# A third shared PSUM bank for the pairs' mixers, and a price for changing the first partition on VectorE and ScalarE in the order model

## The chip, the core and the metric

One core of a Trainium2 chip. The metric is the device time of one execution in microseconds (us). The kernel is written with a list scheduler of its own: Python code keeps a model of when each engine is free and when each result is ready, and it emits every engine's instructions in the order that this model picks. On the chip each engine runs its list in that fixed order and waits where a result isn't there yet.

## The reference, cut to what matters

One layer of a hybrid decoder, for 528 prompt rows (16 meta rows and 512 tokens) and 64 sample rows (8 sequences of 8). All inputs are fp32.

```python
z = einsum('btd,dn->btn', x, w_in)               # 2048 -> 4224 + 4096 columns
o_a, s_a, shift = rwkv7_mixer(z[..., :4224])      # 16 heads x 64: token shift, decay, scan over time, group norm, gate
o_b, s_b = retention_mixer(z[..., 4224:])         # 8 heads x 128: rotary, blocks of 128, group norm, gate
h = einsum('btc,cd->btd', concat([o_a, o_b]), w_out)
y = layer_norm(ALPHA * x + h)
```

The outputs are y for prompt and sample rows, the two mixers' final states, and the last projected rows. The scan of the first mixer is computed in chunks of 64 rows: inside a chunk with matmuls and a triangular inverse, and from chunk to chunk with a recurrence on a 64 x 64 state for each head.

## The kernel before, in words

**Projections.** The work goes by eight pairs p. Pair p takes two heads of the first mixer (units k, r, v, g of kind A) and one head of the second (units q, k, v, g of kind B). A unit is 128 columns of w_in for all 592 rows: 16 contraction tiles of 128, two halves of the rows (272, 258 or 256 columns, then 320), and three matmuls each (high x high, high x low, low x high parts of the fp32 values). So a unit has 96 projection matmuls and a pair 768. They read weights `wh`, `wl` (high and low part of a weight chunk) and `XH`, `XL` (those of x), and write `pj`, PSUM banks 0 and 1. In the lists the eight banks are named bank_115 to bank_122, so bank_115 and bank_116 are the projections'. Each chunk of weights, 128 x 512, comes by DMA into `raw`, ScalarE writes `wh` from it, and VectorE writes `wl` = raw - wh.

**Mixers between the projections.** The mixers' own matmuls are put between the projection matmuls, one small group at a time. Generators write them step by step: `gen_a` (first mixer, up to the chunks), `gen_c` (its recurrence over nine chunks, inside gen_a), `gen_u` (inverse of 32 x 32 blocks, VectorE with DMA), `gen_s` (sample rows), `gen_f` (group norm and gate), `gen_b` (second mixer). `act`, `tt`, `stt` and `ts` are the ScalarE and VectorE instructions, and every one of them has line 363 in the profile, every matmul line 386, and every transpose line 392. Names of tiles tell them apart:
- The recurrence (`gen_c`) does for each chunk c: ScalarE `SF` (two halves of 64 partitions), matmul AR x Y, ScalarE `RHS` (two halves), matmul TT x RHS, VectorE product with `N` into ZZ, matmul BT x ZZ, and VectorE, twice on 64 partitions, the next Y from `bank,FT,SF`. These three matmuls are called the Y step, the RHS step and the BT step below. They alone are a chain: each waits for ScalarE or VectorE work on the result of the one before.
- `gen_s` has eight ScalarE copies into `RSv`, each of 64 partitions, then the transpose `CT,RSv`, and later two matmuls of 64 x 512.
- `gen_b` has eight ScalarE copies of 32 partitions (`XH<-RT` and `RT<-RT`) ahead of two matmuls `XH 128x512` whose contraction has 96 rows.
- `gen_a` begins with the matmuls `LWw` and `LWa` (decay and gain), which need two banks for the two halves of the rows, each written twice and read by ScalarE in between.

**What sets the order.** `Order` holds a clock for each engine and, for each piece of memory, when it is written and read. `Op.ns` is an instruction's cost in the model: for ScalarE 51 ns (input in PSUM) or 93 ns plus 0.833 ns a column, for VectorE 68 ns plus 1.04 ns a column, and more for operands that are pointers. `ready` adds a lag for each dependence: 150 ns from VectorE and 180 ns from ScalarE, and `SLACK` more when the instruction that waits is a matmul. After every projection matmul `pump` looks at the jobs that are live, in order of priority, and puts out each job's next instructions: a mixer's matmul only when the model has its operands ready by now. `ensure` forces what the next projection can't do without.

**Banks.** `take` waits until the list `free` holds as many banks as asked for, and `give` puts them back. `free` begins with m0 and m1 (bank_117 and bank_118). sq (bank_119) serves the first transposes and, at the end, the first output cell; ob (bank_120) is the recurrence's output; r0 and r1 (bank_121 and 122) are gen_b's.

**Output.** After the pairs, w_out is applied in 20 cells of 128 rows x 512 columns, the first of them in bank_119, and the layer norm follows.

Of the kernel before, what the change touches and what calls it, by code (L numbers as in the profile page):

```python
# [28 lines left out]
NPAIR = 8  # L29
RAW_BUFS = 3  # L30
HI_BUFS = 4
SLACK = 200.0
AHEAD = -300.0
RUN = 1200.0
DRAIN = 90.0
LAND = 2400.0
LAND_BIG = 2400.0
LD = 4
# [4 lines left out]
SHARE = "ggggggggggggggdddddd"  # L43
LATE = 5
EARLY = 14
BACKLOG = {0: 4000.0, 1: 1000.0, 2: 500.0, 3: 300.0, 4: 100.0}

_CSPEC = [("ident", 128), ("ind", 2), ("mS", 64), ("mSs", 64), ("mQ", 64), ("mQs", 64),
# [62 lines left out]
class Op:  # L111


    __slots__ = ("eng", "ns", "reads", "writes", "emit", "size")

    def __init__(self, eng, ns, reads, writes, emit, size=None):
        self.eng, self.ns, self.emit, self.size = eng, ns, emit, size
        self.reads, self.writes = [_box(a) for a in reads], [_box(a) for a in writes]


def _box(ap):


    t = ap.tensor
    dims = ap.ap
    if ap.space == bass.MemoryType.DRAM:
        return (t.name, 0, 1, ap.offset, ap.offset + sum((n - 1) * abs(s) for s, n in dims) + 1)
    if ap.space == bass.MemoryType.PSUM:
        return (t.name, -1, 0, 0, 1)
    pitch = 1  # L130
    for d in t.shape[1:]:
        pitch *= d
    p0, c0 = divmod(ap.offset, pitch)
    return (t.name, p0, p0 + dims[0][1], c0, c0 + sum((n - 1) * abs(s) for s, n in dims[1:]) + 1)


def _is_ap(x):
# [19 lines left out]
class Order:  # L157
# [6 lines left out]
    def __init__(self):  # L164
        self.clock = {k: 0.0 for k in ("PE", "DVE", "ACT", "POOL", "SP", "AQ", "DMA")}
        self.mem = {}
        self.job = None
        self.live = []
        self.stage = {}
        self.first = 0.0  # L170
        self.shape = (128, 128)
        self.tiles = [[0.0, 0.0] for _ in range(16)]
        self.issued = (0.0, 0.0)

    def lag(self, src, dst, raw):
        if src == dst:
            return 130.0 if raw and src in ("DVE", "ACT", "POOL") else 0.0
        return self.LAG[src] + SLACK * (dst == "PE")

    def ready(self, op):  # L180
# [7 lines left out]
                        t = max(t, end + self.lag(eng, op.eng, w and not isw))  # L188
        return t

    def emit(self, op):
        ns = op.ns
        start = max(self.clock[op.eng], self.ready(op))
        end = start + ns
        if op.eng == "PE":
            end = self.array(op, self.ready(op))
        self.clock[op.eng] = end
        if op.eng in ("SP", "AQ"):
            end = max(end + 1300.0, self.clock["DMA"]) + op.size / 270.0
            self.clock["DMA"] = end  # L200
            end += LAND if op.size < 2e5 else LAND_BIG
        for boxes, w in ((op.reads, False), (op.writes, True)):
            for n, p0, p1, c0, c1 in boxes:
                l = self.mem.setdefault(n, [])
                if len(l) > 40:
                    t = self.clock["PE"] - 3000.0
                    l[:] = [x for x in l if x[6] > t]
                l.append((p0, p1, c0, c1, w, op.eng, end))
        op.emit()

    def array(self, op, ready):
# [4 lines left out]
        if shape != self.shape:  # L216
            idle = max(e for _, e in self.tiles) + DRAIN
            for x in self.tiles:
# [68 lines left out]
    def pump(self):  # L287
        more = True
        limit = self.clock["PE"] + RUN
        while more:  # L290
            more = False
            for j in list(self.live):
                while self.flushed(j):
# [3 lines left out]
                    if op.eng == "PE":  # L297
# [5 lines left out]
                        elif r > now:  # L303
                            break
                    elif r > now + AHEAD - LATER * (j.name == "load") or self.clock[op.eng] > now + BACKLOG[j.prio * (op.eng != "SP")]:
                        break
# [61 lines left out]
class TensorEngine:  # L368
# [3 lines left out]
    def place(self, lhsT, out, whole):  # L372

        _, p0, p1, _, _ = _box(lhsT)
        c0, m = out.offset // out.tensor.shape[1], _cols(lhsT)
        up = lambda n: 32 if n <= 32 else 64 if n <= 64 else 128
        r, c = up(p1 - p0), 128 if whole else up(m)
        return (r, c), [4 * i + j for i in range(p0 // 32, (p0 // 32) + r // 32) for j in range(0 if whole else c0 // 32, (0 if whole else c0 // 32) + c // 32)]
# [28 lines left out]
def kernel(ctx, tc, x_prompt, x_sample, state_rwkv, state_shift, state_ret, meta_tokens, w_in, w_out,  # L407
# [3 lines left out]
    od = Order()  # L411
    V, A, G = (Engine(e, k, od) for e, k in ((nc.vector, "DVE"), (nc.scalar, "ACT"), (nc.gpsimd, "POOL")))
# [133 lines left out]
    bank = [psum.tile([128, 512], F32, name=f"bank{i}") for i in range(8)]  # L546
    pj = [bank[0], bank[1]]
    m0, m1, sq, ob, r0, r1 = bank[2:]
    free = [m0, m1]

    o_d = dram.tile([16, 128, 576], F32, name="o_d")
    lt_d = [dram.tile([4, 10, 32, 32], F32, name=f"lt_d{i}") for i in range(2)]
# [23 lines left out]

    def give(*b):
        od.call(lambda: free.extend(b))

    lock = [1]  # L580

# [419 lines left out]
    def span(u, half):  # L1001

        if half:
            return H0, H1
        t0 = {"A": 14 * (u[2] in "rg"), "B": 16 * (u[2] in "qg"), "L": 0}[u[0]]
        return t0, H0 - t0
# [88 lines left out]
    j_in = len(chunks)  # L1095
    for i in range(EARLY):
        events.append(("out", len(chunks), 0, i, (0, 1)))
        chunks.append(("out", korder[i], 0))
    for n in range(4):
        for i in range(KO):  # L1100
            events.append(("out", len(chunks), n, i, (2, 3, 4) if n == 0 and i < EARLY else tiles))
            chunks.append(("out", korder[i], n))
    j_one = j_in + EARLY + KO
    last = {ev[1]: e for e, ev in enumerate(events)}
# [48 lines left out]
    with tc.manual_schedule():  # L1153
# [192 lines left out]
        for e, ev in enumerate(events):  # L1346
            stage["event"] = e
            j = ev[1]
            if ev[0] == "in":
                _, j, u, half, q, ui = ev  # L1350
                kind, p, s = u
                if half == 0 and q == 0:
                    if kind == "A" and s == "k":
                        od.start(f"A{p}", gen_a(p), 1)
                    if kind == "B" and s == "q":
                        od.start(f"B{p}", gen_b(p), 3)
                if q == 0 and ui:
                    od.ensure("evac", 2 * ui - 1 + half)
                if ui == 0 and half == 1 and q == 0:
                    od.ensure("x", 99)  # L1360
                od.ensure("split", j + 1)
                t0, n = span(u, half)
                b, jb = pj[half], part[j]
                for kk in range(4):
                    kt = 4 * q + kk
                    w = slice(128 * kk, 128 * kk + 128)
                    for i, (a_, x_) in enumerate(((WH[jb], xh), (WH[jb], xl), (WL[jb], xh))):
                        mm(b[:, :n], a_[:, w], x_[:, kt, t0:t0 + n], start=(kt == 0 and i == 0), stop=(kt == 15 and i == 2))
                        if kk == 3 and i == 2:
                            stage["event"] = e + 1  # L1370
                            if q == 3:
                                stage["proj"] = 2 * ui + half + 1
                        od.pump()
            else:
                _, j, n, ki, some = ev
                od.ensure("o", ki + 1)
                if ki == 0:
                    if n == 0 and 4 in some:
                        od.ensure(f"B{NPAIR-1}", 99)
                        od.ensure("shift", 99)  # L1380
                    if n:
                        od.ensure(f"F{NPAIR-1}", 99)
                        od.ensure("cell", 5 * n + 5 - 8)
                od.ensure("split", j + 1)
                work = [(t, ki, part[j]) for t in some]
                if n == 3 and ki >= KO - HELD:
                    late += work[1:]
                    work = work[:1]
                    if ki == KO - 1:
                        work += sorted(late, key=lambda w: w[0])  # L1390
                for iw, (t, k_, jb) in enumerate(work):
                    b = obank[5 * n + t]
                    if k_ == 0 and b in pj:
                        od.ensure("evac", 2 * len(units) - 1 + pj.index(b))
                    tok = slice(128 * t, 128 * t + 128)
                    if t < 4:
                        todo = [(b, xo[:, k_, tok], WH[jb]), (b, xl[:, k_, tok], WH[jb]), (b, xo[:, k_, tok], WL[jb])]
                    else:
                        todo = [(b, xo[:, k_, tok], WH[jb]), (b[0:64], xo[:, k_, 512:576], WL[jb])]
                        if k_ == KO - 1:  # L1400
                            todo.reverse()
                    for i, (b_, x_, w_) in enumerate(todo):
                        end = i == len(todo) - 1
                        mm(b_, x_, w_, start=(k_ == 0 and i == 0), stop=(k_ == KO - 1 and end))
                        if k_ == KO - 1 and end:
                            stage["out"] = 5 * n + t + 1
                        if iw == len(work) - 1 and end:
                            stage["event"] = e + 1
                        od.pump()
# [41 lines left out]
```

## Time and profile before

| | |
|---|---|
| median of 3 runs | 1382.36 us (1382.06 to 1383.02) |
| profiled execution | 1382.55 us, span 1380.8 us |
| TensorE matmul busy | 1331.4 us, 96% of the span |
| TensorE weight load busy | 1230.1 us, 89% |
| VectorE busy | 884.0 us, 64% |
| ScalarE busy | 644.7 us, 47% |
| DMA | 139.79 MB, 101 GB/s in the mean |
| granted TensorE clock | 0.991 in the mean |

PE is the row of the matmuls, PEld that of the weight loads, which run ahead of the matmuls. Their busy times overlap, since a matmul's record lasts longer than the distance to the next one's start. Where PEld is idle and a releaser is named, the array's next weights waited for that engine. The pairs follow each other at 139.2 us. "Position" is used below for a place in TensorE's list: the number of projection matmuls that stand ahead of it in its pair, 0 to 767.

### The profile page before, as it was taken

How to read it: one execution, taken by the hardware profiler on the slowest of the kernel's cores; microseconds unless marked ns; L12 is line 12 of the kernel's file. 1: busy time of each engine (PE TensorE's matmuls, PEld its weight loads, DVE VectorE, ACT ScalarE, POOL GpSimd, SP SyncE). 2: the span in 40 equal slices, each digit the busy share in tenths (PEclk: the TensorE clock that was granted, in tenths of full speed). 3: DMA queues.
4: the chain of work that ended last, by engine and by line, in shares of the span. 5: the costliest groups of instructions: out<-in, count | busy, mean ns of one | idle time of the engine just before them, and what ended most of it. 6: DMA issues, size and time to landing. Idle time of an engine off the chain costs nothing.

```text
span 1380.8 us, 26964 instructions
## 1 busy us (share of the span) xinstructions
PE 1331.4 (96%) x10392; PEld 1230.1 (89%) x10392; DVE 884.0 (64%) x2158; ACT 644.7 (47%) x1519; POOL 72.5 (5%) x131
## 2 busy tenths in 40 slices
PE   7999999999999999999999999999999999999993
PEld 6999899989998999899989998999899987777782
DVE  5774677566766676667666765676567658624347
ACT  4534564366336633663356435643564366512121
POOL 0000000000000000000000000100010001000024
PEclk9999999999999999999999999999999999999997
DMA  7343224322432243224322432243224347654313
GB/s 238 87 109 90 69 74 118 94 66 72 118 87 73 66 123 85 75 65 120 84 81 64 118 80 81 63 118 85 80 62 120 88 138 214 195 166 117 98 48 122
DMA packets 232342, 139.79 MB, mean 101 GB/s; under 512 B 58668, under 2 KB 212102, under 8 KB 231238
## 3 DMA queue, kind: packets, MB, share of 16 engines
q1 hardware_dynamic: 232214, 138.08, 35.3%
q8 instruction: 81, 1.33, 0.4%
q14 instruction: 47, 0.39, 0.1%
HBM read 119.30 MB, written 18.74 MB: 100 GB/s over the span
## 4 chain that ended last, share of the span: by engine, by line
PE 81%; DVE 9%; ACT 6%; issue 3%; DMA 0%; POOL 0%; DVEq 0%; SPq 0%; ACTq 0%; POOLq 0%
PE bank L386 77%; DVE RW L363 5%; PE bank L392 4%; DVE wl L363 1%; ACT RW L363 1%; ACT SF L363 1%; ACT XH L363 1%; DVE MOM L363 1%; ACT RT L363 1%; ACT RHS L363 1%; ACT wh L363 1%; DVE RT L363 1%; ACT RSv L363 1%; DVE SHT L363 1%; DVE XL L363 0%
## 5 line engine op out<-in xcount | busy, mean ns | idle before, releaser
L386 PE MATMUL bank<-XH,wl 128*128 128x320 f32 (+3 forms) x2080 | 634.0, 305 | 2.1 <-DVE wl L363 2.1
L386 PE MATMUL bank<-XL,wh 128*128 128x320 f32 (+3 forms) x2080 | 629.1, 302 | 0.0
L386 PE MATMUL bank<-XH,wh 128*128 128x320 f32 (+3 forms) x2080 | 627.5, 302 | 1.2 <-ACT wh L363 1.2
L386 PEld LDWEIGHTS bank<-XL,wh 128*128 128x128 f32 x2080 | 391.9, 188 | 7.9 <-issue 6.3
L386 PEld LDWEIGHTS bank<-XH,wl 128*128 128x128 f32 x2080 | 392.9, 189 | 6.0 <-DVE wl L363 3.6
L386 PEld LDWEIGHTS bank<-XH,wh 128*128 128x128 f32 x2080 | 392.8, 189 | 3.0 <-ACT wh L363 1.4
L363 DVE TENSOR_TENSOR wl<-raw,wh 128x512 fp32r<-128x512 f32 x292 | 201.4, 691 | 203.0 <-ACT wh L363 200.1
L363 ACT ACTIVATE wh<-raw 128x512 fp32r<-128x512 f32 x292 | 184.1, 631 | 205.3 <-PE bank L386 178.6
L363 DVE TENSOR_TENSOR RW<-RW 120x84 f32<-120x84 f32 (+27 forms) x558 | 149.9, 272 | 19.5 <-ACT RW L363 4.0
L386 PE MATMUL bank<-RW 32*32 32x32 f32 (+6 forms) x1904 | 146.8, 242 | 2.9 <-DVE RW L363 2.0
L386 PEld LDWEIGHTS bank<-RW 32*32 32x32 f32 (+4 forms) x1904 | 108.9, 145 | 28.0 <-DVE RW L363 9.0
L363 ACT ACTIVATE RW<-bank 128x512 f32<-128x512 f32 (+8 forms) x218 | 93.2, 438 | 47.2 <-PE bank L392 33.3
L363 ACT ACTIVATE RT<-bank 64x320 f32<-64x320 f32 (+9 forms) x122 | 47.7, 398 | 126.4 <-DVE RT L363 102.7
L363 ACT ACTIVATE SF<-RW,FT 64x64 f32<-64x64 f32 x144 | 49.7, 345 | 71.1 <-DVE RW L363 69.2
L386 PE MATMUL bank<-more,XH 128*128 128x512 f32 (+1 forms) x250 | 75.9, 395 | 0.0
L363 ACT ACTIVATE RW<-bank,OMM 128x272 f32<-128x272 f32 (+1 forms) x66 | 33.2, 502 | 68.9 <-PE bank L386 67.4
L386 PE MATMUL bank<-wh,XH 128*128 128x512 f32 x157 | 62.0, 396 | 0.0
L392 PE MATMUL bank<-CT,RW 128*128 128x128 f32 (+2 forms) x348 | 53.7, 282 | 8.2 <-DMA RW<-in_x_prompt_dram 7.5
L386 PE MATMUL bank<-wl,XH 128*128 128x512 f32 (+1 forms) x157 | 61.6, 394 | 0.0
L386 PEld LDWEIGHTS bank<-more,XH 128*128 128x128 f32 (+1 forms) x250 | 45.6, 183 | 12.4
L363 DVE TENSOR_TENSOR RW<-bank,N 64x128 f32<-64x128 f32 x80 | 22.5, 282 | 46.8 <-PE bank L386 45.7
L392 PEld LDWEIGHTS bank<-CT,RW 128*128 128x128 f32 (+2 forms) x348 | 41.2, 139 | 10.4 <-issue 7.5
(154 smaller groups left out, 1397.3 us busy)
## 6 DMA issues: line engine op xcount, KB each, us to landing
raw<-in_w_in_dram SPq DMA_DIRECT2D x259, 256.0 KB
raw<-in_w_out_dram SPq DMA_DIRECT2D x48, 256.0 KB
CT<-in_w_out_dram SPq DMA_DIRECT2D x30, 256.0 KB
RT<-in_state_ret_dram SPq DMA_DIRECT2D x8, 512.0 KB
out_dram<-RT SPq DMA_DIRECT2D x8, 512.0 KB
RW<-in_x_prompt_dram SPq DMA_DIRECT2D x16, 256.0 KB
out_dram<-RW SPq DMA_DIRECT2D x16, 256.0 KB
RW<-o_d SPq DMA_DIRECT2D x14, 288.0 KB
```

The costliest lines, as they stand in the source:

```text
L363: self.order.submit(Op(self.key, self.cost(name, n, kw, psum), reads, [out], lambda: f(*args, **kw)))
L386: lambda: self.eng.matmul(out, lhsT, rhs, start=start, stop=stop), (passes, move, load, shape, tiles)))
L392: lambda: self.eng.transpose(out, in_, ident), (1, move, _cols(in_) / 1.2, shape, tiles)))
```

## The change

It has three parts. `free` begins with three banks, so the mixers may also hold sq, and a job `keep` takes that bank out of the list from the last pair's unit g on, before the output phase writes it. In the model, an instruction on VectorE or ScalarE starts 110 ns later (`SWITCH`) than its engine is free when the first partitions of its output and first input aren't those of the engine's instruction before. And `SLACK`, the extra lag ahead of every matmul, goes from 200 to 100 ns. No instruction is added or removed: the model puts the same ones in another order.

```diff
-SLACK = 200.0
+SLACK = 100.0
...
+SWITCH = 110.0
...
+KEEP = ("A", 7, "g")
...
     def __init__(self, eng, ns, reads, writes, emit, size=None):
         self.eng, self.ns, self.emit, self.size = eng, ns, emit, size
+        self.rows = tuple(_row(a) for a in writes + reads[:1])
...
+def _row(ap):
+    pitch = 1
+    for d in ap.tensor.shape[1:]:
+        pitch *= d
+    return ap.offset // pitch
...
+    def switch(self, op):
+
+        return SWITCH * (op.eng in ("DVE", "ACT") and self.rows.get(op.eng) != op.rows)
+
     def emit(self, op):
         ns = op.ns
-        start = max(self.clock[op.eng], self.ready(op))
+        start = max(self.clock[op.eng] + self.switch(op), self.ready(op))
+        self.rows[op.eng] = op.rows
...
-    free = [m0, m1]
+    free = [m0, m1, sq]
...
+    def gen_keep(b):
+
+        while not any(x is b for x in free):
+            yield
+        free[:] = [x for x in free if x is not b]
+        yield
...
+                    if (kind, p, s) == KEEP:
+                        od.start("keep", gen_keep(sq), 0)
...
+                od.ensure("keep", 99)
```

**First place: ScalarE and TensorE in the last unit of pair 3.** ScalarE's list from the copy of the sample state (`RW<-bank 128x512`) on, before:

```order
L363 ACTIVATE RW<-bank_117 128x512
L363 ACTIVATE RT<-bank_121,CT 32x128
L363 ACTIVATE XH<-RT 32x128 x2
L363 ACTIVATE RT<-RT 32x128 x2
L363 ACTIVATE XH<-RT 32x128 x2
L363 ACTIVATE RSv<-bank_117 64x4x8
L363 ACTIVATE RT<-RT 32x128 x2
L363 ACTIVATE RSv<-bank_117 64x4x8 x2
L363 ACTIVATE wh_102<-raw_101 128x512
```

The same place after the change:

```order
L380 ACTIVATE RW<-bank_119 128x512
L380 ACTIVATE RT<-bank_121,CT 32x128
L380 ACTIVATE RT<-bank_115 128x256
L380 ACTIVATE XH<-RT 32x128 x2
L380 ACTIVATE RSv<-bank_119 64x4x8
L380 ACTIVATE RT<-RT 32x128 x2
L380 ACTIVATE RSv<-bank_119 64x4x8
L380 ACTIVATE XH<-RT 32x128 x2
L380 ACTIVATE RSv<-bank_119 64x4x8
L380 ACTIVATE SF<-RW,FT_83 64x64
L380 ACTIVATE wh_102<-raw_101 128x512
```

The copies themselves stand much as they did, a little more mixed; the sample rows now use the third bank. What moved is TensorE's list, where the matmuls that wait for them stand. Before, in the second weight chunk of that half unit (wh_103), from position 741 on:

```order
L386 MATMUL bank_121<-XH 128x512
L386 MATMUL bank_118<-RW 128x128
L386 MATMUL bank_116<-XH,wh_103 128x320
L386 MATMUL bank_116<-XL,wh_103 128x320
L392 MATMUL bank_117<-CT,RSv 128x128
L386 MATMUL bank_116<-XH,wl_107 128x320
L386 MATMUL bank_116<-XH,wh_104 128x320
L386 MATMUL bank_116<-XL,wh_104 128x320
L386 MATMUL bank_118<-RHS,RW 66x128
```

After, in its fourth chunk (wh_105), from position 758 on:

```order
L403 MATMUL bank_118<-RHS,RW 66x128
L403 MATMUL bank_121<-XH 128x512
L403 MATMUL bank_116<-XH,wl_109 128x320
L403 MATMUL bank_116<-XH,wh_105 128x320
L403 MATMUL bank_116<-XL,wh_105 128x320
L403 MATMUL bank_116<-XH,wl_109 128x320
L403 MATMUL bank_118<-RW 128x128
L403 MATMUL bank_119<-CT,RSv 128x128
```

The XH matmul went from position 741 to 758, the RSv transpose from 743 to 762, and the RHS step of that chunk from 746 to 758.

**Second place: TensorE at the next pair's LWw matmuls.** Before, they come right after the recurrence's last group (`64x64 x32`), at position 97:

```order
L386 MATMUL bank_120<-RW 64x64 x32
L386 MATMUL bank_115<-XH,wh_102 128x258
L386 MATMUL bank_117<-LWw,WHw 128x272
L386 MATMUL bank_117<-LWw,WLw 128x272
L386 MATMUL bank_118<-LWw,WHw 128x320
L386 MATMUL bank_118<-LWw,WLw 128x320
```

After, they come at position 45, while the recurrence still runs in bank_118 (RW 128x128 is a step of it):

```order
L403 MATMUL bank_119<-RW 64x512 x2
L403 MATMUL bank_115<-XL,wh_105 128x272
L403 MATMUL bank_115<-XH,wl_109 128x272
L403 MATMUL bank_118<-RW 128x128
L403 MATMUL bank_117<-LWw,WHw 128x272
L403 MATMUL bank_117<-LWw,WLw 128x272
L403 MATMUL bank_115<-XH,wh_105 128x272
L403 MATMUL bank_115<-XL,wh_105 128x272
L403 MATMUL bank_119<-LWw,WHw 128x320
L403 MATMUL bank_119<-LWw,WLw 128x320
```

The LWw matmuls moved 52 positions forward; the recurrence's end (`64x64 x32`) moved from position 96 back to 145, and the transposes of its result for the group norm (`bank_120<-CT,RW 128x128 x4`) from 172 to 245. The two matmuls of 64x512, which stood at positions 9 and 10, now stand together at 43. TensorE's last 645 instructions, all of them in the output phase, stand as before.

More of the change, by code (lines that the diff above doesn't have):

```diff
@@ L111 @@
 class Op:
-    __slots__ = ("eng", "ns", "reads", "writes", "emit", "size")
+    __slots__ = ("eng", "ns", "reads", "writes", "emit", "size", "rows")
     def __init__(self, eng, ns, reads, writes, emit, size=None):
         self.eng, self.ns, self.emit, self.size = eng, ns, emit, size
+        self.rows = tuple(_row(a) for a in writes + reads[:1])
         self.reads, self.writes = [_box(a) for a in reads], [_box(a) for a in writes]
@@ L173, in __init__ @@
         self.issued = (0.0, 0.0)
+        self.rows = {}
     def lag(self, src, dst, raw):
```

## The prediction

> **What bounds the kernel now.** The page first: the engines' busy shares and the chain that ended last.
>
> ```profile
> span 1380.8 us, 26964 instructions
> PE 1331.4 (96%) x10392; PEld 1230.1 (89%) x10392; DVE 884.0 (64%) x2158; ACT 644.7 (47%) x1519; POOL 72.5 (5%) x131
> PE 81%; DVE 9%; ACT 6%; issue 3%; DMA 0%; POOL 0%; DVEq 0%; SPq 0%; ACTq 0%; POOLq 0%
> ```
>
> TensorE is the bound: 81% of the chain is its own. A new order of the same instructions can gain only what TensorE loses by waiting. The table by stretches shows where that is.
>
> ```profile
> 517.80:552.30 34.50, 34.50 (x254) 34.50 (x253) 21.74 (x64) 12.33 (x25) 0.00 (x0) 1.00 0.32 85
> 552.00:691.20 139.20, 137.24 (x1166) 130.06 (x1165) 92.94 (x242) 69.79 (x172) 5.15 (x11) 1.00 0.32 86
> 691.20:830.40 139.20, 137.26 (x1166) 130.08 (x1165) 92.92 (x242) 69.81 (x172) 5.15 (x11) 1.00 0.32 87
> ```
>
> Columns: stretch, length, then PE, PEld, DVE, ACT and POOL busy, granted clock, DMA. The two long rows are one pair each, and alike to 0.02 us: the order repeats, and so do its waits. In the first row, where projections run and mixers hardly touch TensorE, the weight loads fill all 34.50 us. In a pair they leave 139.20 - 130.06 = 9.14 us open, and the matmuls 1.96. The clock is 1.00, so nothing is lost to that. Next, the waits in that pair: releaser, total us, times, longest.
>
> ```profile
> PEld bank L386 <- issue: 2.1, 8, 0.8
> PEld bank L386 <- DVE wl L363: 1.3, 2, 0.8
> PEld bank L386 <- ACT RHS L363: 1.3, 4, 0.4
> PEld bank L386 <- DVE RW L363: 1.0, 3, 0.4
> PEld bank L386 <- ACT wh L363: 1.0, 1, 1.0
> PEld bank L392 <- ACT RSv L363: 0.6, 1, 0.6
> PEld bank L386 <- ACT RW L363: 0.2, 1, 0.2
> ```
>
> Without `issue`, which is TensorE's own and stays, 5.4 us a pair are waits for ScalarE and VectorE. No row names a DMA. The same question for the second pair's stretch (135.3 to 274.4, the first three rows) and for the end of the last pair with the early output cells (1108.8 to 1182.6, the other four):
>
> ```profile
> PEld bank L386 <- ACT RHS L363: 2.1, 3, 1.4
> PEld bank L386 <- DVE RW L363: 1.4, 4, 0.8
> PEld bank L392 <- ACT RSv L363: 0.7, 1, 0.7
> ...
> PEld bank L386 <- ACT RHS L363: 2.3, 5, 0.6
> PEld bank L386 <- DVE RW L363: 2.2, 4, 0.9
> PEld bank L386 <- ACT XH L363: 0.6, 1, 0.6
> PEld bank L392 <- ACT RSv L363: 0.6, 1, 0.6
> ```
>
> That is 4.2 and 5.7 us. With six stretches of 5.4 the change can work on 42.3 us of waiting in all.
>
> **What a wait costs.** One RHS step that waited 0.23 us, in order of time:
>
> ```profile
> 593.24 0.31 PE L386 MATMUL bank<-XH,wl 128*128 128x320 f32 x1
> 593.39 0.38 PE L386 MATMUL bank<-RW 128*128 128x128 f32 x2
> 593.76 0.31 PE L386 MATMUL bank<-XL,wh 128*128 128x320 f32 x1
> 594.12 0.45 ACT L363 ACTIVATE RHS<-bank 64x64 f32<-64x64 f32 x2
> 594.34 0.31 PE L386 MATMUL bank<-XH,wl 128*128 128x320 f32 x1
> 594.62 0.19 PEld L386 LDWEIGHTS bank<-RHS,RW 128*66 128x66 f32 x2 [0.23 <-ACT RHS L363]
> 595.04 0.31 PE L386 MATMUL bank<-XL,wh 128*128 128x320 f32 x1
> ```
>
> From 593.76 to 594.34 stand four projection matmuls, 0.145 us each. From 593.24 to 593.76 the Y step's two passes and two projections take 0.52, so a step costs 0.23 by itself. From 594.34 to 595.04 the same mix with the wait takes 0.70: a wait of 0.23 costs 0.18, four fifths. I use 0.8. So the ceiling is 42.3 x 0.8 = 34 us.
>
> **The price (SWITCH), first place.** ScalarE during the wait of 1.0 us at the XH matmul and 0.6 at the RSv transpose:
>
> ```profile
> 568.29 0.60 ACT L363 ACTIVATE RW<-bank 128x512 f32<-128x512 f32 x1
> 569.30 0.64 ACT L363 ACTIVATE XH<-RT 32x128 fp32r<-32x128 f32 x2
> 571.28 0.19 ACT L363 ACTIVATE RSv<-bank 64x32 f32<-64x32 f32 x1
> 572.01 0.39 ACT L363 ACTIVATE RSv<-bank 64x32 f32<-64x32 f32 x2
> 572.42 0.63 ACT L363 ACTIVATE wh<-raw 128x512 fp32r<-128x512 f32 x1
> 573.67 0.28 ACT L363 ACTIVATE RSv<-bank 64x32 f32<-64x32 f32 x2
> 574.50 0.46 ACT L363 ACTIVATE RHS<-bank 64x64 f32<-64x64 f32 x2
> ```
>
> ScalarE is saturated from 568.29 to 574.96. Two RSv take 0.39 us at 572.01, where the first partition changes between them, and 0.28 at 573.67, where it doesn't: 0.11 apart. The model's cost of an RSv is 78 ns against 0.19 here, of a 32x128 copy 200 ns against 0.32. So it thought these sixteen copies done nearly 2 us too early and put the XH matmul and the transpose there. That is SWITCH's 110 ns.
>
> [...]
>
> After: from the end of the 0.60 copy at 568.89 to the end of RHS at 574.96 ScalarE now takes 6.07 us. In the new list stand in that stretch one more `wh` (0.63) and a 128x256 copy (some 0.3, between the 0.19 and 0.60 rows by columns), and three RSv fewer (-0.4): 6.6 us. TensorE fills the time from the group of 64x32 matmuls to the RHS step at position 758 with 33 projections (4.8 us), a BT and a Y step (0.46) and that group:
>
> ```profile
> 569.18 0.66 PE L386 MATMUL bank<-RW 128*64 128x32 f32 x16
> 569.77 0.41 PE L386 MATMUL bank<-XH,wl 128*128 128x320 f32 x1
> ```
>
> 0.66 us, so 5.9 of 6.6: some 0.5 of wait is left, of 1.6. Four projections (0.6 us) and two more matmuls separate it from the RSv transpose, whose last copies take 1.1: nothing more is lost there. Term: 1.1 us a pair.
>
> **The RHS steps.** RHS began at 594.12, 0.3 us late, behind other ScalarE work, and six projections stood between Y and RHS step. In the new list it is 8 or 10 at positions 53, 74, 108 and 127, which gives 1.4 to 1.7 us from the Y step's start against the 1.23 measured here (593.39 to 594.62); at 694 and 722, where 5 and 3 stand, four two-pass matmuls of gen_b or gen_s fill in (0.9 us). Of 1.3 us I leave 0.3. Term: 1.0.
>
> **DVE RW.** These are BT and Y steps and the 64x512 matmuls behind VectorE. Steps on 64 partitions get the price too, and the second 64x512 still stands close behind its operand. I take half. Term: 0.5.
>
> **DVE wl.** The longest wait is at the unit v:
>
> ```profile
> 622.78 0.76 DVE L363 TENSOR_TENSOR RW<-N2b,CT 64x576 f32<-64x576 f32 x1
> 623.56 0.69 DVE L363 TENSOR_TENSOR wl<-raw,wh 128x512 fp32r<-128x512 f32 x1
> ```
>
> wl stands behind gen_a's products on halves of partitions. In VectorE's new list these stand a chunk and more earlier (the N2b product is two `wl` ahead). Between no change and 1.3 I take 0.8, since one of two waits is 0.8.
>
> **The smaller SLACK.** It takes 0.1 us of margin from each group that waits, some 30 a pair. Where the producer changes partitions, SWITCH gives 0.11 back for each instruction, and most chains have two. Bounds: 0 and 30 x 0.1 = 3.0 us; nearest to the chains with two switches, so 0.3. The page has no row for a margin.
>
> **The third bank.** LWw and LWa at position 45 put ScalarE's tanh work among the recurrence, which ends 49 positions later. TensorE does the same work, and what waits for the recurrence is gen_f, whose deadline is priced below. [...] SP's DMAs and POOL's instructions keep their queues, with gen_f's store 73 positions later; nothing on TensorE waits for either in the list above.
>
> **Sum.** 1.1 + 1.0 + 0.5 + 0.8 - 0.3 = 3.1 us of waiting, times 0.8 = 2.5 us for each of six stretches: 15.0. The second pair by share (4.2 of 5.4): 1.9. The last stretch, with the 5.7 us mostly in RHS and DVE RW, where longer recurrences also meet the output's 512-column matmuls: half, 5.7 x 0.5 x 0.8 = 2.3. Total 19.2 us. Span 1380.8 - 19.2 = 1361.6; the profiled execution lies 1.75 above its span and 0.2 above the median, so 1363.2.
>
> **Rivals.**
> - *Margins too thin.* SLACK at its bound and no repair of wl and DVE RW: 1.1 + 1.0 - 1.5 = 0.6 x 0.8 x 8 = 4 us: 1372 to 1380 with the mixtures between. For it: 0.1 us is less than one projection. Against: prices now match the durations. 0.17.
> - [...] 0.08.
> - *Slower: gen_f too late.* The unit v's projections end at position 288, and unit g's first matmul there needs bank_115 read out into zsV, which gen_f still reads. Its transposes moved from 172 to 245: 43 positions, 6.2 us. After them ScalarE has four copies of 64x256 and three `wh` (0.63):
>
> ```profile
> L363 ACT ACTIVATE RW<-bank,GSW 64x256 f32<-64x256 f32 x16 | 9.0, 564 | 0.4
> ```
>
> 4 x 0.56 + 3 x 0.63 + two copies out of the bank (0.9) = 5.1. Spare 1.1 us, and more by mixers' groups in between. If gen_f ran 1.1 + 2.5 = 3.6 us later than this, the gain would be gone; at 5 us later each of seven pairs loses 1.4: 1392. Against: no DMA or POOL wait stands in that chain except the group norm's power on POOL. 0.08.
> - *Better.* Nearly all 34 us: 1346 to 1350. 0.07.
>
> **How the numbers follow.** The forecast, 1350 to 1372, has 0.60. A measurement tells about 0.2% (2.8 us) from no change. Faster: 0.60 + 0.17 + 0.07 = 0.84; same 0.08; slower 0.08. The range from 1348 to 1381 leaves out the slower case, most of the unchanged one and the best end; the likeliest case's own is 1350 to 1372.
>
> **What the profile after would show.** PEld waits of a pair at 2 to 3 us instead of 5.4, RSv's gone and `ACT wh` under 0.6; RHS under 0.5; a pair at 136.5 us with PEld still about 130 busy; TensorE's instruction count the same. Wrong if a pair's new waits name `RW<-bank,VEC`, zsV's copies or many short ones of 0.1 (SLACK), or if the stretch after the last pair grows.

## The result, and the profile after

The changed kernel takes 1359.85 us (median of 4 runs, 1356.94 to 1360.47) against 1382.69 (1382.06 to 1383.52) for the kernel before: a ratio of 0.983, 95% interval 0.9813 to 0.9847. The forecast was 1363.2, so the time lies 3.4 us below it and in the range. Two of its terms were wrong by more than that, in opposite directions.

The head of the page after: the span, the engines' busy time, and the chain that ended last.

```profile
span 1357.2 us, 26984 instructions
PE 1318.2 (97%) x10392; PEld 1225.5 (90%) x10392; DVE 880.9 (65%) x2158; ACT 645.2 (48%) x1519; POOL 75.3 (6%) x131
PE 89%; DVE 7%; issue 2%; ACT 1%; DMA 1%; POOL 0%; SPq 0%; DVEq 0%; POOLq 0%
```

TensorE's share of the chain rises from 81% to 89%, ScalarE's falls from 6% to 1%. The count of matmuls is the same and the busy times hardly move. It is the same work with fewer waits, as a new order must be. In the profile after, ScalarE's and VectorE's line 363 is L380, matmuls are L403 and transposes L409.

A pair after, in the table by stretches, and its waits for weights (releaser, total us, times, longest); the next pair has the same waits:

```profile
566.00:701.40 135.40, 135.15 (x1168) 129.52 (x1166) 92.33 (x242) 69.93 (x172) 5.75 (x11) 1.00 0.33 89
...
PEld bank L403 <- issue: 1.9, 7, 0.8
PEld bank L403 <- DVE RW L380: 1.4, 4, 0.7
PEld bank L403 <- DVE wl L380: 0.4, 1, 0.4
PEld bank L409 <- DVE RW L380: 0.2, 1, 0.2
PEld bank L403 <- ACT RHS L380: 0.2, 1, 0.2
```

A pair went from 139.2 to 135.4 us. Without `issue` the waits fell from 5.4 to 2.2 us. RSv and `wh` are gone from the list, RHS is down from 1.3 to 0.2 and `wl` from 1.3 to 0.4. DVE RW grew, from 1.0 to 1.6. These are the releasers' names; where the waits stand, and what they wait for, differs from the names at one place, and the account behind the experiments goes by place.

Where the 23.6 us of span come from can be read at one instruction that each pair has, the first RSv copy. From pair to pair its starts are 140.0, five times 139.2, and 136.6 us apart before, and 134.4, 136.8, four times 135.4, and 134.0 after. First and last of them, before and then after (line, copies, durations in ns, first and last start):

```profile
L363 ACT ACTIVATE RSv<-bank x8: 177/185/194, 152.8 to 153.8; 64x32 f32<-64x32 f32 x8
L363 ACT ACTIVATE RSv<-bank x3: 168/178/192, 1125.5 to 1126.4; 64x32 f32<-64x32 f32 x3
L380 ACT ACTIVATE RSv<-bank x4: 176/190/191, 152.9 to 153.9; 64x32 f32<-64x32 f32 x4
L380 ACT ACTIVATE RSv<-bank x2: 191/191/191, 1099.7 to 1100.8; 64x32 f32<-64x32 f32 x2
```

Up to 152.8 nothing changed (+0.1). The seven distances shrank from 972.7 to 946.8, by 25.9 us. What follows the last one grew from 1380.8 - 1125.5 = 255.3 to 1357.2 - 1099.7 = 257.5, by 2.2. The sum is 23.6. The end of the last pair with the early output cells shows the growth (1083.0 to 1156.8, the same place in the program as 1108.8 to 1182.6 before, whose rows the prediction shows):

```profile
PEld bank L403 <- DVE RW L380: 3.2, 8, 0.8
PEld bank L403 <- issue: 3.0, 7, 0.8
PEld bank L403 <- ACT RHS L380: 2.5, 5, 1.5
PEld bank L403 <- DVE XL L380: 2.0, 4, 0.8
```

DVE RW went from 2.2 to 3.2, and XL, on which output cells wait, is new with 2.0: with the rows of 0.6 us and less of both, 5.9 us became 8.7. Of the 3.2, 0.8 are a matmul group's own time (the account below shows one like it), so XL is the main growth. When the changed list is built, the planner puts out 26 instructions by force ahead of three weight chunks of the output, and none in the list before (force is explained below). Whether the waits on XL come from that was not tested.

### The profile page after: what moved, and what is told of

It reads as the page before. It is cut to its first block, busy times and chain, and to the rows that moved or that the text cites. A ratio compares the mean times of both kernels' runs of the same rounds, so it can differ in the third digit from the quotient of the medians.

```text
span 1357.2 us, 26984 instructions
## 1 busy us (share of the span) xinstructions
PE 1318.2 (97%) x10392; PEld 1225.5 (90%) x10392; DVE 880.9 (65%) x2158; ACT 645.2 (48%) x1519; POOL 75.3 (6%) x131
## 4 chain that ended last, share of the span: by engine, by line
PE 89%; DVE 7%; issue 2%; ACT 1%; DMA 1%; POOL 0%; SPq 0%; DVEq 0%; POOLq 0%
PE bank L403 85%; PE bank L409 4%; DVE RW L380 3%; DVE wl L380 1%; DVE MOM L380 1%; DVE SHT L380 1%; DMA RW<-in_x_prompt_dram 0%; DVE XL L380 0%; DMA RW<-o_d 0%; ACT RW L380 0%; DVE RT L380 0%; ACT XH L380 0%; ACT SF L380 0%; POOL SHT L380 0%; ACT RT L380 0%
## 5 line engine op out<-in xcount | busy, mean ns | idle before, releaser
L403 PE MATMUL bank<-XH,wl 128*128 128x320 f32 (+3 forms) x2080 | 629.1, 302 | 1.6 <-DVE wl L380 1.6
L403 PE MATMUL bank<-XL,wh 128*128 128x320 f32 (+3 forms) x2080 | 629.3, 303 | 0.0
L403 PE MATMUL bank<-XH,wh 128*128 128x320 f32 (+3 forms) x2080 | 627.5, 302 | 1.2 <-ACT wh L380 1.2
L403 PEld LDWEIGHTS bank<-XH,wl 128*128 128x128 f32 x2080 | 392.5, 189 | 6.0 <-DVE wl L380 3.1
L403 PEld LDWEIGHTS bank<-XL,wh 128*128 128x128 f32 x2080 | 391.9, 188 | 5.9 <-issue 5.0
L403 PEld LDWEIGHTS bank<-XH,wh 128*128 128x128 f32 x2080 | 392.7, 189 | 4.5 <-ACT wh L380 1.4
L380 DVE TENSOR_TENSOR wl<-raw,wh 128x512 fp32r<-128x512 f32 x292 | 200.9, 689 | 188.1 <-ACT wh L380 183.9
L380 ACT ACTIVATE wh<-raw 128x512 fp32r<-128x512 f32 x292 | 183.7, 630 | 168.7 <-PE bank L403 148.9
L380 DVE TENSOR_TENSOR RW<-RW 120x84 f32<-120x84 f32 (+27 forms) x558 | 150.3, 273 | 22.1 <-ACT RW L380 4.3
L403 PE MATMUL bank<-RW 32*32 32x32 f32 (+6 forms) x1904 | 143.8, 242 | 1.6 <-DVE RW L380 1.1
L403 PEld LDWEIGHTS bank<-RW 32*32 32x32 f32 (+4 forms) x1904 | 105.4, 145 | 25.9 <-DVE RW L380 11.8
L380 ACT ACTIVATE RW<-bank 64x256 f32<-64x256 f32 (+8 forms) x218 | 93.1, 439 | 57.4 <-PE bank L409 35.5
L380 ACT ACTIVATE RT<-bank 64x320 f32<-64x320 f32 (+9 forms) x122 | 47.6, 397 | 122.8 <-DVE RT L380 102.9
L380 ACT ACTIVATE SF<-RW,FT 64x64 f32<-64x64 f32 x144 | 49.7, 345 | 59.9 <-DVE RW L380 57.5
L403 PE MATMUL bank<-more,XH 128*128 128x512 f32 (+1 forms) x250 | 75.9, 395 | 0.0
L403 PE MATMUL bank<-wh,XH 128*128 128x512 f32 x157 | 62.3, 398 | 0.0
L409 PE MATMUL bank<-CT,RW 128*128 128x128 f32 (+2 forms) x348 | 54.1, 284 | 8.4 <-DMA RW<-in_x_prompt_dram 7.8
L403 PE MATMUL bank<-wl,XH 128*128 128x512 f32 (+1 forms) x157 | 61.7, 395 | 0.0
L380 ACT ACTIVATE RW<-bank,OMM 128x272 f32<-128x272 f32 (+1 forms) x66 | 33.3, 505 | 51.5 <-PE bank L403 49.1
L403 PEld LDWEIGHTS bank<-more,XH 128*128 128x128 f32 (+1 forms) x250 | 45.6, 183 | 12.5
L409 PEld LDWEIGHTS bank<-CT,RW 128*128 128x128 f32 (+2 forms) x348 | 41.5, 140 | 11.3 <-issue 7.8
L403 PE MATMUL bank<-wh,XL 128*128 128x512 f32 x126 | 50.5, 401 | 0.6 <-DVE XL L380 0.6
```

The source lines that it names most:

```text
L380: self.order.submit(Op(self.key, self.cost(name, n, kw, psum), reads, [out], lambda: f(*args, **kw)))
L403: lambda: self.eng.matmul(out, lhsT, rhs, start=start, stop=stop), (passes, move, load, shape, tiles)))
L409: lambda: self.eng.transpose(out, in_, ident), (1, move, _cols(in_) / 1.2, shape, tiles)))
```

## The experiments

The change has three parts: the price SWITCH, the third bank, and SLACK 100 for 200. All experiments are made from the changed kernel. Theories A, B and C in the first four say that the price, the bank or the margin carries the gain.

### The parts alone

The price alone:

```
-SLACK = 100.0          +SLACK = 200.0
-free = [m0, m1, sq]    +free = [m0, m1]    (and no keep)
```

> The order before with SWITCH 110 alone (two shared banks, SLACK 200). Theory A, that the waits before came from unpriced changes of the first partition: 1362 to 1372 us, and a pair's waits for RHS, RSv and the XH matmul fall as in the whole change. Theory B, that the third bank carries the gain: within 4 us of before (1379 to 1387). Theory C, that the smaller SLACK carries it: also near before, or slower by a few us, since margin and price add up.

The bank alone:

```
-SLACK = 100.0          +SLACK = 200.0
-SWITCH = 110.0         +SWITCH = 0.0
```

> The order before with the third bank and keep alone (no price, SLACK 200). Theory A: 1377 to 1387 us, a pair's waits for RHS, RSv and XH as before (about 5 us). Theory B: 1358 to 1368. Theory C: near before.

The margin alone, and the margin with the price:

```
-SWITCH = 110.0         +SWITCH = 0.0       (slack_only; price_slack keeps 110)
-free = [m0, m1, sq]    +free = [m0, m1]    (and no keep)
```

> The order before with SLACK 100 alone (no price, two banks). Theory A: slower, 1385 to 1400 us, because the margin that covered part of the missing price is halved: up to 0.1 us more of wait in each of some 30 groups a pair. Theory B: slower or the same. Theory C: 1358 to 1370.

> The whole change without the third bank (SWITCH 110, SLACK 100, two banks). Theory A: 1357 to 1364 us, as the whole change. Theory B: 1375 or more. Theory C: as A, so this run tells only the bank from the other two.

Measured, with the kernel before at 1382.69 us beside them: price 1406.40 (ratio 1.0176, 1.0161 to 1.0191), bank 1386.78 (1.0029, 1.0017 to 1.0041), margin 1400.68 (1.0134, 1.0117 to 1.0151), price and margin 1394.26 (1.0085, 1.007 to 1.01). Each is slower than before, while all three together are 23 us faster. Some expectations were met (A's 1377 to 1387 for bank_only, B's "slower or the same" for slack_only and "1375 or more" for price_slack), but each theory fails where it names the part that carries the gain. Theories A, B and C fall as they stand: no part carries it by itself.

In the price-only kernel the waits at which the price was aimed do shrink, and one place goes bad. A pair's waits for VectorE and ScalarE, then the end of unit v of another pair, stretch by stretch:

```profile
PEld bank L403 <- DVE RW L380: 5.9, 3, 3.1
PEld bank L403 <- ACT RW L380: 1.0, 2, 0.8
PEld bank L403 <- ACT RHS L380: 0.4, 1, 0.4
PEld bank L409 <- DVE RW L380: 0.3, 1, 0.3
...
349.00:358.00 9.00, 5.06 (x43) 4.60 (x41) 8.83 (x18) 3.68 (x8) 0.96 (x3) 0.97 0.30 87
358.00:370.00 12.00, 9.96 (x56) 8.73 (x57) 7.69 (x20) 1.08 (x4) 0.29 (x2) 0.60 0.15 49
```

RHS is at 0.4 and RSv is gone, but three waits on VectorE, of up to 3.1 us, take 5.9. In 349 to 358 TensorE is busy for 5.06 of 9 us and VectorE for 8.83. Behind that the granted clock falls to 0.60. The margin-only kernel keeps a clock of 1.00 in a pair and loses in more and shorter waits instead: DVE RW has 3.9 us in seven waits of at most 1.0, RHS 1.4 in four.

### The parts with the bank, and a double price

With these two the eight combinations of the parts are complete; the third doubles the price.

```
bank_price:  -SLACK = 100.0     +SLACK = 200.0
bank_slack:  -SWITCH = 110.0    +SWITCH = 0.0
switch220:   -SWITCH = 110.0    +SWITCH = 220.0
```

> The changed kernel with SLACK back at 200: the third bank and the price, no smaller margin. Theory D (the third bank makes the price pay: with two banks the priced, longer chains of gen_a come late for the unit behind them and TensorE is made to stand in front of them, 2 to 3 us a place; with three it is not): the long waits at the 64x128 matmuls on RW are gone, the small waits of a pair are 2 to 3 us, 1358 to 1372 us. Theory E (no part has a meaning of its own; each list is another throw, and the changed kernel is a lucky one): anywhere from 1375 to 1410, with new long waits at some group. Theory C (the smaller SLACK carries the gain): 1378 us or more, with waits of many groups as before.

> The changed kernel with SWITCH 0: the third bank and the smaller margin, no price. Theory D: the margin is taken and nothing is put in its place, so the short waits on DVE RW and ACT RHS grow: 1386 to 1400 us, slower than the kernel before; no long waits at the 64x128 matmuls. Theory E: anywhere from 1360 to 1410. Theory C: 1358 to 1370 us.

> The changed kernel with SWITCH 220 for 110. Theory D: the model now thinks ScalarE and VectorE slower than they are, chains are put further apart than they need, and long chains come late for their units again: 1362 to 1385 us, the loss in a few long waits on DVE RW, not in many short ones. Rival (more margin is better): 1350 to 1358 us. Theory E: anywhere from 1360 to 1410.

Measured, with the kernel before at 1382.56: bank and price 1398.39 (1.0117, 1.0099 to 1.0135), bank and margin 1380.38 (0.9985, 0.9975 to 0.9994), double price 1393.21 (1.0068, 1.0043 to 1.0094). Theory D said that the third bank is enough to make the price pay, and that bank_slack is slower than before; both are refuted, and switch220 is above its range too. C falls with bank_slack. Theory E, every list a throw, fits all three but names no cause. bank_price is 38.5 us slower than the changed kernel though only SLACK differs. The same place in it, in order of time:

```profile
356.20 0.71 PE L403 MATMUL bank<-RW 64*128 64x128 f32 x6 [0.56 <-DVE RW L380]
358.27 2.45 PE L409 MATMUL bank<-CT,RW 128*128 128x128 f32 x10 [1.36 <-DVE RW L380]
361.86 0.58 PE L403 MATMUL bank<-XH,wh 128*128 128x258 f32 x1 [1.14 <-ACT RW L380]
362.24 0.42 PE L403 MATMUL bank<-XL,wh 128*128 128x258 f32 x1
362.45 0.42 PE L403 MATMUL bank<-XH,wl 128*128 128x258 f32 x1
...
366.18 0.28 PE L403 MATMUL bank<-XH,wl 128*128 128x258 f32 x1
366.30 0.28 PE L403 MATMUL bank<-XH,wh 128*128 128x258 f32 x1
```

Unit v's projections are over, and unit g's first one (the 128x258 at 361.86) can't start before unit v is read out of its bank. Between them stand chunk matmuls of gen_a and transposes, with nothing to fill the waits. After them 258-column matmuls come at 0.21 us each (362.24 to 362.45) where they take 0.12 some 4 us later: the granted clock is 0.50 from 358.36 to 365.19 (row in the last section).

The code says why. Here unit g asks for the evacuation of unit v, and that waits for gen_f of the pair before, which still reads zsV:

```
main loop:  if q == 0 and ui: od.ensure("evac", 2 * ui - 1 + half)
gen_evac:   yield from until((f"A{p-1}", 1 if s == "k" else 3) if s in "kr" else (f"F{p-1}", 99))
```

When the planner reaches unit g before gen_f is done, `ensure` emits by force, with no look at what TensorE will wait for, what comes next of all jobs until gen_f and the evacuation are through. That is the prediction's slower rival, gen_f too late. How many instructions a list has there can be counted while it is built. It isn't a time, but it sorts the kernels:

| kernel | SWITCH | banks | SLACK | by force at such a place (places) | mean clock | us |
|---|---|---|---|---|---|---|
| before | 0 | 2 | 200 | 0 | 0.991 | 1382.4 to 1383.0 |
| slack_only | 0 | 2 | 100 | 0 | 0.992 | 1400.68 |
| bank_only | 0 | 3 | 200 | 0 | 0.993 | 1386.78 |
| bank_slack | 0 | 3 | 100 | 0 | 0.991 | 1380.38 |
| price_only | 110 | 2 | 200 | 37 or 38 (7) | 0.975 | 1406.40 |
| price_slack | 110 | 2 | 100 | 35 to 39 (4) | 0.977 | 1394.26 |
| bank_price | 110 | 3 | 200 | 38 (6), 14 (1) | 0.974 | 1398.39 |
| switch220 | 220 | 3 | 100 | 15 to 56 (7) | 0.977 | 1393.21 |
| changed kernel | 110 | 3 | 100 | 0 | 0.991 | 1359.85 |

The four with a forced place are the four with a lowered clock (0.974 to 0.977 against 0.991 to 0.993). Of the five without, the one with the price is 20.5 us faster than the best of the others, bank_slack, from which it differs in the price alone. Neither the third bank nor the smaller margin is enough to avoid the place: bank_price and switch220 have three banks, price_slack and switch220 the margin of 100.

### What a change of first partitions costs

Ten groups of 24 instructions of 64x32, five on ScalarE and then five on VectorE, stand behind the output and write a tile that nobody reads after. `outs` and `ins` are the first partitions that output and input take in turn:

```
+for outs, ins in (((0,), (0,)), ((0, 64), (0, 64)), ((0, 64), (0,)), ((0,), (0, 64)), ((64,), (0,))):
+    go(24, outs, ins)
```

> The changed kernel with ten added groups of 24 instructions of 64x32 behind the output, copies on ScalarE and sums on VectorE, into a tile that nobody reads after: (1) first partition 0 for output and input, (2) both alternate between 0 and 64, (3) only the output alternates, (4) only the input alternates, (5) output constantly 64 and input constantly 0. Read from the spacing of starts within a group. Theory of the price: (1) and (5) alike, (2) dearer by about 110 ns an instruction on both engines, (3) and (4) dearer as well. Rival (the 0.11 us of the two RSv is something else of that place): all five alike within 20 ns.

The table by stretches, cut at each group's first start, ScalarE's five and then VectorE's (length of the stretch, the engine's busy time and count, clock, DMA):

```profile
1337.24:1340.10 2.86, 2.86 (x24) 0.58 0.03 10
1340.10:1345.83 5.73, 5.45 (x25) 0.50 0.12 46
1345.83:1351.59 5.76, 5.48 (x24) 0.50 0.30 96
1351.59:1357.35 5.76, 5.48 (x24) 0.50 0.66 224
1357.35:1360.21 2.86, 2.85 (x24) 0.50 0.00 0
...
1353.88:1356.33 2.45, 2.45 (x24) 0.50 0.67 217
1356.33:1361.12 4.79, 4.47 (x26) 0.50 0.00 0
1361.12:1365.87 4.75, 4.42 (x24) 0.50 0.01 2
1365.87:1370.64 4.77, 4.43 (x25) 0.50 0.00 0
1370.64:1373.09 2.45, 2.45 (x24) 0.50 0.00 0
```

Its one time, 1376.33 us, includes these groups. A count of 25 or 26 takes in a neighbour at the cut; each group has 24. On ScalarE an instruction takes 2.86 / 24 = 0.119 us with the partitions kept, also where output and input differ but stay (fifth row), and 5.76 / 24 = 0.240 with both alternating, or either alone: 121 ns more. On VectorE it is 0.102 and 0.199: 97 ns. So the price is real, the rival (all alike within 20 ns) is refuted, and 110 is close to the mean of the two. What the engines do in that time, no run shows.

### Taking the forced place away

One number of bank_price is changed:

```
 SLACK = 200.0
-od.call(lambda: od.start(f"F{p}", gen_f(p), 2))
+od.call(lambda: od.start(f"F{p}", gen_f(p), 1))
```

> The third bank and the price at SLACK 200, as in bank_price, with one number changed: gen_f runs at priority 1 instead of 2. Theory G (what made the four lists with the price slow is one place: the evacuation of unit v waits for gen_f of the pair before, the planner reaches unit g without it and emits the whole tail of gen_a and gen_f by force, TensorE stands in front of it, and its clock falls to half): with gen_f ahead the planner emits 2 instructions by force there in every second pair instead of 38 in each, so the long waits and the low clock go, and 25 to 38 us with them: 1360 to 1374 us. Rival H (SLACK 200 with the price is slow in itself, since every chain is spread too far): 1390 to 1400 us.

It ran in 1359.49 us (1357.9 to 1360.17; ratio 0.9831, 0.9817 to 0.9846, with 1382.95 before): 38.9 us faster than bank_price, the same as the changed kernel, and 0.5 below theory G's range. By force it has 6 instructions at one place and 4 at three others; the "2" of the expectation was a miscount. Bank_price has a span of 1396.4 us and a mean clock of 0.974, this one 1356.0 and 0.992. The same place in each (bank_price first, this one second), then a pair of bank_price and two of this one, whose pairs alternate:

```profile
357.00:366.00 9.00, 6.59 (x32) 5.83 (x33) 4.67 (x13) 2.91 (x7) 0.29 (x2) 0.62 0.56 155
349.00:358.00 9.00, 9.00 (x76) 8.61 (x75) 7.19 (x18) 3.25 (x8) 0.29 (x2) 1.00 0.51 139
...
575.00:716.00 141.00, 137.78 (x1168) 131.56 (x1168) 92.13 (x241) 69.89 (x173) 5.05 (x11) 0.98 0.31 86
559.20:695.50 136.30, 136.30 (x1176) 130.66 (x1175) 93.11 (x244) 70.89 (x177) 5.49 (x11) 1.00 0.32 89
695.50:829.40 133.90, 133.15 (x1156) 128.39 (x1156) 91.68 (x239) 68.52 (x169) 6.84 (x11) 1.00 0.33 90
```

Where bank_price had a clock of 0.62 and 32 matmul instructions in 9 us, this one has 1.00 and 76. So SLACK 200 with the price isn't slow in itself (rival H); the forced place is. The clock's share has a bound: (1 - 0.974) x 1396.4 = 36.3 us of clock missing in bank_price, (1 - 0.992) x 1356.0 = 10.8 here, 25.5 between them. That counts low clock under waits too, so at most 25.5 of the 40.4 us of span are the clock's, and the other 15 or more are the waits' and the order's.

Three more kernels have nothing forced at that place: a smaller margin, two banks at half the price, and the price as measured.

```
slack50:         -SLACK = 100.0    +SLACK = 50.0
two_banks_half:  SWITCH = 55.0, SLACK = 50.0, free = [m0, m1]    (and no keep)
measured_price:  -SWITCH = 110.0   +SWITCH = {"ACT": 121.0, "DVE": 97.0};  SLACK = 60.0
```

> The changed kernel with SLACK 50: third bank, price 110, and nothing emitted by force inside the pairs. Theory G (a list with the price and without the forced place is good; the margin itself is worth little): 1355 to 1370 us, waits of a pair 2 to 4 us, most of them short ones on DVE RW. Rival I (the margin counts, each 0.05 us of it taken from some 30 waits of a pair): 1367 to 1380 us.

> The kernel before's two banks, SWITCH 55 and SLACK 50: a list with half the price, two banks and nothing emitted by force inside the pairs. Theory G: the third bank is needed only to get past the forced place; half the price gives about half of the 20 us that lie between bank_slack and the changed kernel: 1366 to 1380 us. Rival J (two banks hold the mixers back by themselves, whatever the price): 1383 to 1400 us, with waits on DVE RW as in slack_only.

> The changed kernel with the price as rowcost measured it, 121 ns on ScalarE and 97 on VectorE, and SLACK 60, at which nothing is emitted by force inside the pairs. Theory G: as good as the changed kernel in the pairs, 1352 to 1366 us; a better price moves little, since 110 is the mean of the two. Rival E (each list is another throw): anywhere from 1360 to 1400 us.

Measured: slack50 1360.64 (0.9845, 0.983 to 0.9859), two_banks_half 1375.41 (0.9953, 0.9937 to 0.997), measured_price 1360.06 (0.9836, 0.9822 to 0.9851). All three lie where theory G has them; measured_price alone would also fit the lower edge of rival E. Two banks don't hold the mixers back whatever the price (rival J): a pair of two_banks_half (569.6 to 707.8) has 138.2 us, with 1.3 us of waits on RHS and 1.2 on DVE RW. That half the price gives about half the gain isn't shown by it, since bank and margin differ too. The whole price with two banks ran only in lists with the forced place; two banks with gen_f ahead were not run, so whether the third bank is needed then stays open.

The four lists with a price of about 110 and the place (nearly) free are within 1.2 us of each other: 1359.49, 1359.85, 1360.06, 1360.64. Each list is another order, so rival E (every list a throw) has little left: with the price and without the place four lists agree, while the four without either (before, slack_only, bank_only, bank_slack) lie between 1380 and 1401. None beats the changed kernel by more than runs of one kernel differ. Their pairs take 135.1 to 135.6 us in the mean of two, and weight loads alone fill 129.5 of that. What is left to an order is small.

## Why the prediction was right, and where its terms were not

- **TensorE as the bound, and the ceiling in its waits: right.** The waits of a pair fell to 2.2 us where 5.4 - 3.1 = 2.3 was forecast. The terms behind it go by place below.
- **The price at XH and RSv: right, undersized.** Of the two waits (1.0 and 0.6) 0.2 is left in a steady pair, at the RHS step right ahead of the XH matmul: 1.3 us went, 1.1 was forecast. ScalarE took 6.5 us from the end of its 128x512 copy (693.46) to the end of RHS, against the estimate of 6.6; TensorE's own work, from the 64x32 group at 693.71, took 6.1 against 5.9.

```profile
699.71 0.22 ACT L380 ACTIVATE RHS<-bank 64x64 f32<-64x64 f32 x1
699.98 0.20 PEld L403 LDWEIGHTS bank<-RHS,RW 128*66 128x66 f32 x2 [0.22 <-ACT RHS L380]
```

- **RHS: right, undersized.** All four waits of the pair before are gone (the 0.2 named RHS after is the one just shown): 1.3 instead of 1.0.
- **DVE wl: the step that failed.** The prediction puts the longest wait on `wl`, 0.8, at the unit v, and lets it go because `wl` comes sooner there. At the unit v the wait was 0.47, and 0.38 is left (first two rows, before and after): 0.1 went, not 0.8. The wait of 0.81 stands at another place, behind a 64x512 group (four rows before, three after):

```profile
624.31 0.19 PEld L386 LDWEIGHTS bank<-XH,wl 128*128 128x128 f32 x1 [0.47 <-DVE wl L363]
610.40 0.19 PEld L403 LDWEIGHTS bank<-XH,wl 128*128 128x128 f32 x1 [0.38 <-DVE wl L380]
...
582.03 0.19 PEld L386 LDWEIGHTS bank<-RW 128*64 128x64 f32 x2 [0.41 <-DVE RW L363]
583.03 0.30 PEld L386 LDWEIGHTS bank<-RW 128*128 128x128 f32 x2 [0.81 <-DVE wl L363]
583.58 0.19 PEld L386 LDWEIGHTS bank<-RW 128*64 128x64 f32 x2
584.58 0.19 PEld L386 LDWEIGHTS bank<-XL,wh 128*128 128x128 f32 x1 [0.81 <-issue]
...
574.33 0.19 PEld L403 LDWEIGHTS bank<-RW 128*64 128x64 f32 x2 [0.17 <-DVE RW L380]
575.24 0.19 PEld L403 LDWEIGHTS bank<-RW 128*64 128x64 f32 x2 [0.72 <-DVE RW L380]
576.24 0.19 PEld L403 LDWEIGHTS bank<-XL,wh 128*128 128x128 f32 x1 [0.81 <-issue]
```

  Behind each 64x512 group the next weights of another shape come 1.00 us after the group's own, with 0.81 idle, whether the name is `wl` or `issue`. So this 0.81 was the group's own time and no wait for `wl`: a named releaser is the last one that the profile saw, not always the one that was waited for. Of the 5.4 us, 4.6 were waits for other engines.
- **DVE RW: right in size, by place.** By name it grew from 1.0 to 1.6 where half was to go. By place, the two 64x512 groups had 0.41 and 0.81 between them and now, standing together, have 0.17 and 0.72, in which the second waits for VectorE's product (574.51 to 575.18): 0.3 less. The forecast has no term for this move. The recurrence's steps on RW went from 0.6 to 0.3, so 0.6 us went in all where 0.5 was forecast. New are two waits of 0.2 at later matmuls on RW; one of 0.2 on ACT RW went, which I had left out.
- **The sum: right because errors cancel.** XH and RSv, RHS, `wl`, DVE RW, ACT RW and the two new waits give 1.3 + 1.3 + 0.1 + 0.6 + 0.2 - 0.4 = 3.1, the forecast's number, with `wl` too high by 0.7 and most other terms too low. That is luck.
- **SLACK at -0.3: not shown as a cost.** With price and bank, 100 and 50 take the same time (1359.85 and 1360.64), and 200 does too once gen_f goes ahead (1359.49). Without the price it moved the time by +18.0 us with two banks and -6.4 with three. It has no fixed price. Whether the two new waits on RW are the smaller margin stays open.
- **0.8 us for each us of wait: mis-sized.** A pair shrank by 3.8 us for 3.2 of waits, so 1.2. The open time of the weight loads fell from 9.14 to 5.88, by 3.3, which is the waits at full price. The other 0.5 is the loads' own busy time, 130.06 to 129.52. One form stands out, the forty loads of 64x128 on RW: at 187 ns each they filled 2.9 us before and 2.5 after, so more of them overlap each other. Why was not tried. My factor came from one RHS step, where 0.05 of a wait of 0.23 us was caught up with; no second wait was measured, and the totals say that most aren't caught up with.
- **Sum over the stretches.** The pairs gave 25.9 us against a forecast 15.0 + 1.9 = 16.9, the end lost 2.2 against a gain of 2.3. The net error of 4.4 us is small because the two have opposite signs. The end's term had no mechanism behind it, only "half".
- **The third bank, without a term: wrong reasoning.** I asked what its waits cost, not what the planner can do without it. Two banks with the price of 110 met the forced place in both lists that ran, and cost 12 to 24 us against before; price_slack, which lacks only the bank, is 34.4 us slower than the changed kernel.
- **The rivals.** *gen_f too late* (0.08, 1392) didn't happen here, but is the mechanism of four other lists, at 1393 to 1406. I found the place and the condition, and missed two things: the planner doesn't only come late there, it stops choosing, and the clock is lower in those lists (0.974 to 0.977 in the mean). A pair of bank_price lost (1398.39 - 1382.56) / 7 = 2.3 us against before, where I had 1.4, and 38.9 / 7 = 5.6 against the list without the place. That a change of first partitions costs nothing is refuted by rowcost (121 and 97 ns). *Margins too thin* and *better* don't describe the pairs.
- **What the profile was to show.** Waits of 2 to 3 us, RSv gone, `wh` under 0.6, RHS under 0.5: all so. A pair at 136.5 with the weight loads still about 130 busy: 135.4 and 129.5. The stretch after the last pair grew, which I had named as a sign of being wrong; it cost 2.2 us.

## What to carry to other kernels

A truer cost can make a list scheduler's chains longer in its model, as the price did here. If a place in the program forces whatever a deadline needs, the longer chains can miss it, and the loss there (5.6 us a pair) exceeds what the truer cost gains (3.8). So count the forced instructions of each list before believing any time, and undo parts of a change only with that count beside them: alone, each of these three parts looked harmful or useless. When a job is late by a hair, a higher priority for it acts on that place; that alone turned 1398 into 1359 us. A margin of 100 did as much in the changed kernel, but not in price_slack and switch220. And before a wait is put into a sum, look at the row in order of time: the releaser's name gave 0.8 us to the wrong cause here.

## What the runs showed of the hardware

- Changing the first partition between 0 and 64, of output and input or of either alone, cost 121 ns an instruction on ScalarE (0.240 us for 0.119) and 97 on VectorE (0.199 for 0.102) at 64x32 in rowcost, which doubles its time.
- Behind a 64x512 group (weights of 128x64) the next weights of another shape came 1.00 us later, with 0.81 us idle, before and after (rows in the account above).
- TensorE's clock fell without a long standstill. In the 3.41 us before the drop in bank_price (first row) matmuls were busy for 1.49, with waits of 0.56 and 1.36 shown above. Then it is at 0.50 for 6.83 us (second row) though TensorE is busy for 5.69 of them. The busy share of such a stretch alone doesn't decide: in bank_only a stretch with 2.06 us of 3.40 kept the clock (third row; 1.00 in the mean of its pair, 568.4 to 708.2), while in another place of bank_price it fell behind 2.10 of 3.41 (fourth row, 494.89 to 498.30; 0.79 in the mean of 500 to 520). What brings the clock down and up again, these runs don't show.

```profile
354.95:358.36 3.41, 1.49 (x11) 0.92 (x11) 3.27 (x7) 0.63 (x1) 0.00 (x0) 1.00 0.26 77
358.36:365.19 6.83, 5.69 (x25) 4.93 (x26) 3.36 (x10) 2.91 (x7) 0.29 (x2) 0.50 0.68 186
589.80:593.20 3.40, 2.06 (x18) 1.79 (x16) 2.40 (x5) 0.49 (x1) 2.49 (x1) 1.00 0.02 5
494.89:498.30 3.41, 2.10 (x15) 1.52 (x13) 3.24 (x7) 0.72 (x2) 0.00 (x0) 1.00 0.30 87
```
